# Down projection of 12 of 22 FFN pairs from seven block products instead of eight

## The chip, the cores and the metric

The kernel runs on one core of one Trainium2 chip. The metric is device time in microseconds (us) of one execution. The core has TensorE (PE in the profile; its weight loads are PEld), VectorE (DVE), ScalarE (ACT), GpSimd (POOL) and SyncE (SP). Each engine takes its own instructions in a fixed order and waits on semaphores for the others. DMAs are issued from SP's and from ACT's queue.

## The reference

One layer of an encoder block on 512 tokens of width 2048, all float32: an attention half (two branches, gates, output projection, LayerNorm) and a feed-forward half. The change is in the latter:

```python
h = modulate(layer_norm(x), shift2, scale2)
f = (jax.nn.silu(h @ w_ffn_gate[l]) * (h @ w_ffn_up[l])) @ w_ffn_down[l]
x = layer_norm_affine(DEEPNORM_ALPHA * x + gate2 * f, ln2_g[l], ln2_b[l])
```

Gate and up are 2048 x 5632, down is 5632 x 2048.

## The kernel before

**Split operands.** Each float32 operand is cut into a high part h (a cast to fp32r on ACT, line 95) and a low part l (the difference, on DVE, line 96). A product is three matmuls: h*h, h*l and l*h (`mm3`, lines 77 to 79). So every weight passes SP's DMA into a `raw` tile, a cast on ACT into a `wh` tile and a subtraction on DVE into a `wl` tile before TensorE can use it. `raw`, `wh` and `wl` have four buffers each, taken in turn.

**Gate and up.** The 5632 hidden columns are handled as 22 pairs of 128. For pairs 2 to 21 the products with gate and then with up are made by `strassen`, with seven block products in the place of eight (Winograd's form). A call has four steps (u = 0 to 3), each with 512 rows of weights, and a step has 42 matmuls of 128x256. The first 18 of them use raw blocks of the weights (tiles `hr`, `lr`, lines 1055 and 1056). The other 24 use sums of blocks, which POOL makes in a `tt` tile (lines 1058 to 1060) and which go through `wh` and `wl`. A pair has two calls, 336 matmuls. `combine` (lines 1088 to 1092) adds the products out of PSUM, on DVE but for one copy. After up, line 1138 multiplies silu(gate) by up into `eg` (128x1024: the pair's 256 hidden columns by 512 tokens), and `store_hid` writes that to DRAM from ACT's queue.

**Down.** Pairs 0 to 19 are taken in groups of four: `load_hid` loads a pair's hidden block again and splits it. For each of four column chunks of 512, four PSUM banks (one for each 128 tokens) collect the four pairs, 24 matmuls of 128x512 to a pair and chunk, so 96 to a pair. `drain` multiplies the bank by `gate2` and adds it to the residual `x2`. The last two pairs (N_LAST) have their weights multiplied by `gate2` beforehand, are kept split in SBUF, and run token block by token block, so that the final LayerNorm overlaps them.

**Order.** The program is written in sequence and a list scheduler, which runs a timeline of its own, then sets the order on each engine. That order is fixed when the kernel is built. An instruction behind another one on its engine waits for it.

## Time and profile before

| | |
|---|---|
| median of 3 runs | 2667.63 us (2666.36 to 2672.69) |
| the profiled execution | 2664.01 us, of which the profile's span is 2662.0 us |
| matmul instructions | 15563 |
| PE busy | 2592.6 us, 97% of the span |
| gate and up by seven products | from about 1360 to about 2165 us |
| down | from about 2165 us to the end |

Busy time of PE counts pipelined matmuls that overlap, so the share says where PE has no work, not how near it is to its peak. The rate of matmuls in a stretch says more: instructions of one shape at equal distances mean that nothing holds PE up. PE's clock as granted by the throttle is 1.00 (2.4 GHz) in nearly all slices.

### The profile page before, as it was taken

The page shows a single profiled execution, that of the slowest core. Times are in us where ns is not written, and L with a number is a line of the kernel's source. Part 1 is how long each engine was busy: PE and PEld are TensorE (multiplying, and loading weights), DVE is VectorE, ACT ScalarE, POOL GpSimd, SP SyncE. Part 2 cuts the span into 40 slices and gives each one's busy share as a digit, 9 for nine tenths or more (in the row PEclk, how much of TensorE's full clock was granted, in tenths as well). Part 3 has the DMA queues.
Part 4 walks back from the last instruction along what each step waited for, and adds up shares of the span by engine and source line. Part 5 has one row for each costly group of instructions (what it writes and reads, how often), then busy time and mean ns, then how long its engine had stood idle before and what let it go on. Part 6 is the DMA issues. An engine that isn't in the chain of part 4 may idle for free. (4 is left out here: it accounts for less than half of the span.)

```text
span 2662.0 us, 40015 instructions
## 1 busy us (share of the span) xinstructions
PE 2592.6 (97%) x15563; PEld 2314.5 (87%) x15563; DVE 1833.2 (69%) x2244; ACT 1012.9 (38%) x1456; POOL 1206.8 (45%) x1033
## 2 busy tenths in 40 slices
PE   5999999999989999999899999999999999999998
PEld 4888888789878888888899999999999998888886
DVE  8886787874678644577777677777777755445566
ACT  3332433333344533346644443444444432212321
POOL 0008778876745011020368777776677720000023
PEclk8999999999999999999999999999999999999999
DMA  9976578775734444768753333333333364334442
GB/s 350 320 256 211 156 228 254 244 246 173 237 101 151 129 144 142 240 217 260 238 166 120 118 120 119 115 120 124 111 120 123 116 214 150 119 110 128 151 127 87
DMA packets 330798, 456.11 MB, mean 171 GB/s; under 512 B 19656, under 2 KB 208480, under 8 KB 330096
## 3 DMA queue, kind: packets, MB, share of 16 engines
q1 hardware_dynamic: 307840, 414.77, 49.3%
q10 hardware_dynamic: 22768, 38.78, 4.1%
q8 instruction: 122, 2.00, 0.3%
q14 instruction: 68, 0.56, 0.1%
HBM read 418.87 MB, written 34.62 MB: 170 GB/s over the span
## 5 line engine op out<-in xcount | busy, mean ns | idle before, releaser
L96 DVE TENSOR_TENSOR wl<-raw,wh 128x1024 fp32r<-128x1024 f32 (+2 forms) x342 | 446.7, 1310 | 323.0 <-ACT wh L95 321.6
L95 ACT CAST wh<-raw 128x1024 fp32r<-128x1024 f32 (+2 forms) x342 | 346.3, 1015 | 706.9 <-PE ps_s L79 270.7
L96 DVE TENSOR_TENSOR wl<-tt,wh 128x1024 fp32r<-128x1024 f32 x160 | 235.7, 1474 | 168.3 <-ACT wh L95 168.1
L1058 POOL TENSOR_TENSOR tt<-raw 128x512 f32<-128x512 f32 x160 | 244.2, 1527 | 190.7 <-DMA raw<-in_w_ffn_up_dram 70.0
L95 ACT CAST wh<-tt 128x1024 fp32r<-128x1024 f32 x160 | 167.7, 1049 | 309.4 <-PE ps_s L78 134.5
L1056 DVE TENSOR_TENSOR lr<-raw,hr 128x768 fp32r<-128x768 f32 x160 | 215.4, 1346 | 44.7 <-ACT hr L1055 44.0
L230 POOL TENSOR_TENSOR acc<-acc,tmp 128x512 f32<-128x512 f32 (+1 forms) x154 | 207.3, 1346 | 9.8
L1208 POOL TENSOR_TENSOR raw<-raw,gate 128x512 f32<-128x512 f32 x16 | 25.3, 1609 | 400.9 <-DMA raw<-in_w_ffn_down_dram 400.9
L1055 ACT CAST hr<-raw 128x768 fp32r<-128x768 f32 x160 | 133.6, 835 | 151.0 <-PE ps_s L78 71.4
L226 POOL TENSOR_SCALAR tmp<-braw,csil 128x512 f32<-128x512 f32 x112 | 136.3, 1218 | 117.8 <-DMA braw<-in_w_ada_dram 114.4
L1060 POOL TENSOR_TENSOR tt<-raw,tt 128x256 f32<-128x256 f32 x160 | 174.5, 1092 | 11.7
L1059 POOL TENSOR_TENSOR tt<-raw,tt 128x256 f32<-128x256 f32 x160 | 170.6, 1067 | 11.7
L77 PE MATMUL ps_g<-hTh,wh 128*128 128x512 f32 x384 | 152.1, 397 | 1.7 <-ACT wh L95 1.7
L79 PE MATMUL ps_g<-hTh,wl 128*128 128x512 f32 x384 | 151.0, 394 | 0.0
L78 PE MATMUL ps_g<-hTl,wh 128*128 128x512 f32 x384 | 150.4, 392 | 0.0
L220 DVE SCALAR_TENSOR_TENSOR acc<-braw,csil,acc 128x512 f32<-128x512 f32 x112 | 112.6, 1006 | 43.4 <-DMA braw<-in_w_ada_dram 42.5
L77 PE MATMUL ps_s<-wh,hTh 128*128 128x512 f32 (+1 forms) x384 | 138.1, 361 | 0.0
L77 PE MATMUL ps_s<-sh,wh 128*128 128x256 f32 x480 | 135.2, 282 | 2.7 <-ACT wh L95 2.7
L79 PE MATMUL ps_s<-sh,wl 128*128 128x256 f32 x480 | 136.2, 284 | 1.4 <-DVE wl L96 1.4
L78 PE MATMUL ps_s<-wl,hTh 128*128 128x512 f32 (+1 forms) x384 | 137.5, 358 | 0.0
L79 PE MATMUL ps_s<-wh,hTl 128*128 128x512 f32 (+1 forms) x384 | 137.2, 358 | 0.0
L78 PE MATMUL ps_s<-sl,wh 128*128 128x256 f32 x480 | 136.3, 284 | 0.0
(432 smaller groups left out, 8251.5 us busy)
## 6 DMA issues: line engine op xcount, KB each, us to landing
braw<-in_w_ada_dram SPq DMA_DIRECT2D x128, 512.0 KB, 4.3
raw<-in_w_in_dram SPq DMA_DIRECT2D x96, 512.0 KB, 5.0
...
```

Source lines behind the costliest of these rows:

```text
L77: nc.tensor.matmul(ps, lhsT=ah, rhs=bh, start=start, stop=False)
L78: nc.tensor.matmul(ps, lhsT=ah, rhs=bl, start=False, stop=False)
L79: nc.tensor.matmul(ps, lhsT=al, rhs=bh, start=False, stop=stop)
L95: nc.scalar.copy(out=h[:, :n], in_=src)
L96: nc.vector.tensor_tensor(out=l[:, :n], in0=src, in1=h[:, :n], op=ALU.subtract)
L226: nc.gpsimd.tensor_scalar(out=dst[:, :n], in0=v[:, k, :], scalar1=col, scalar2=1.0, op0=ALU.mult, op1=ALU.mult)
L230: nc.gpsimd.tensor_tensor(out=acc2[:, :n], in0=acc2[:, :n], in1=dst[:, :n], op=ALU.add)
L1055: nc.scalar.copy(out=hr, in_=b[:, :, 1:4, :])
L1056: nc.vector.tensor_tensor(out=lr, in0=b[:, :, 1:4, :], in1=hr, op=ALU.subtract)
L1058: nc.gpsimd.tensor_tensor(out=t[:, :, 0:2, :], in0=b[:, :, 0:1, :].broadcast_to([P, 2, 2, P]), in1=b[:, :, 1:3, :], op=ALU.subtract)
L1059: nc.gpsimd.tensor_tensor(out=t[:, :, 2, :], in0=b[:, :, 2, :], in1=t[:, :, 0, :], op=ALU.subtract)
L1060: nc.gpsimd.tensor_tensor(out=t[:, :, 3, :], in0=b[:, :, 3, :], in1=t[:, :, 2, :], op=ALU.subtract)
```

## The change

**What it does.** Pairs 2 to 13 (`GROUPS`) leave the plain down projection. For them the down product too is made from seven block products: the pair's two blocks of 128 rows, two halves of the tokens and two halves of the output columns (each in two chunks c of 512) are the 2x2 blocks. That is 84 matmuls of 128x512 to a pair instead of 96. It runs over all 12 pairs in four passes: three of the seven products for c = 0, then for c = 1 (`weights1`, six PSUM banks, 18 matmuls to a pair), then the other four for c = 0 and c = 1 (`weights2`, eight banks, 24 matmuls to a pair). At the end of a pass the banks are added into the `x3` tiles without `gate2`; `convert` multiplies by `gate2` and adds the residual later. Pairs 0, 1 and 14 to 19 run as before in two groups (`PLAIN`), the last two as before.

**Weights.** Their block sums are made on DVE, in the loaded tiles: two additions of 128x512 for `weights1`, one of 128x1024 and one of 128x512 for `weights2`; then 1.5 or 2 splits of 128x1024 where a plain pair and chunk has one. Loads go alternately to `raw` tiles and to four new `tp` tiles.

**Activations.** After the multiplication (now line 1189) `hidden_sums` makes the four sums of hidden blocks on POOL (lines 1144 to 1147, into the `eu` tile), splits `eg` and the sums with the same `wh` and `wl` buffers as the weights, and stores the parts by eight DMAs from ACT's queue into `sets_d`. The down passes load them already split (`need1`, `need2`: 0.79 and 1.05 MB a pair) into a ring of 12 tiles.

```diff
+    GROUPS = [[2, 3, 4, 5, 6, 7, 8, 9, 10, 11, 12, 13]]
+    PLAIN = [[0, 1, 14, 15], [16, 17, 18, 19]]
...
+    def half_tile():
+        place[1] += 1
+        if extra_tiles and place[1] > RAW_ONLY and place[1] % 2:
+            return extra_tiles[0].tile([P, 1024], F32, tag="tp", name="tp", bufs=4)
+        return raw_tile()
...
+    def need1(g):
+        tl = set1[g] = ring_tile((3, g))
+        nc.sync.dma_start(out=parts(tl).bitcast(F32)[:, :, 0:768], in_=sets_d[g][:, :, 1024:1792])
...
+    def hidden_sums(g, eg, e):
+
+        nc.gpsimd.tensor_tensor(out=e[:, 0], in0=eg[:, 1], in1=eg[:, 2], op=ALU.subtract)
+        nc.gpsimd.tensor_tensor(out=e[:, 1], in0=e[:, 0], in1=eg[:, 3], op=ALU.subtract)
+        nc.gpsimd.tensor_tensor(out=e[:, 2], in0=eg[:, 3], in1=eg[:, 1], op=ALU.subtract)
+        nc.gpsimd.tensor_tensor(out=e[:, 3], in0=eg[:, 0], in1=e[:, 1], op=ALU.add)
+        for v, moves in ((eg, ((0, 0, 3, 2), (4, 3, 4, 1))), (e, ((2, 2, 4, 1), (5, 0, 2, 1)))):
+            for x, part in enumerate(split(v.rearrange("p b n -> p (b n)"), 1024)):
+                pb = part.bitcast(F32).rearrange("p (b n) -> p b n", b=4)
+                for to, b0, b1, st in moves:
+                    n = (b1 - b0 + st - 1) // st
+                    nc.scalar.dma_start(out=sets_d[g][:, x, to * 256:(to + n) * 256].rearrange("p (b n) -> p b n", b=n), in_=pb[:, b0:b1:st, :])
...
+    def weights1(g, c):
+        a, b = half_tile(), half_tile()
+        av, bv = a.rearrange("p (b n) -> p b n", b=2), b[:, :512]
+        nc.sync.dma_start(out=av, in_=w_rows(g, 0, c))
+        nc.sync.dma_start(out=bv, in_=w_rows(g, 1, c)[:, 1, :])
+        nc.vector.tensor_tensor(out=av[:, 1], in0=av[:, 1], in1=av[:, 0], op=ALU.add)
+        nc.vector.tensor_tensor(out=bv, in0=bv, in1=av[:, 1], op=ALU.add)
+        ah, al = split(a, 1024)
+        bh, bl = split(bv, 512)
...
         nc.vector.tensor_tensor(out=eg, in0=eg, in1=eu, op=ALU.mult)
-        store_hid(g, eg)
...
+        if g in by_sums:
+            hidden_sums(g, eg, eu)
+        else:
+            store_hid(g, eg)
...
-        return bank("ssssgtgt"[(turn8[0] - 1) % 8])
...
+        return bank("ssssggtt"[(turn8[0] - 1) % 8])
...
+    def weights2(g, c):
+        a, b = half_tile(), half_tile()
+        av, bv = a.rearrange("p (b n) -> p b n", b=2), b.rearrange("p (b n) -> p b n", b=2)
+        nc.sync.dma_start(out=bv, in_=w_rows(g, 0, c))
+        nc.sync.dma_start(out=av, in_=w_rows(g, 1, c))
+        nc.vector.tensor_tensor(out=bv, in0=bv, in1=av, op=ALU.add)
+        nc.vector.tensor_tensor(out=bv[:, 0], in0=bv[:, 0], in1=bv[:, 1], op=ALU.add)
+        ah, al = split(a, 1024)
+        bh, bl = split(b, 1024)
...
+    def products(pairs, sets, weights, c, step):
+        bk = None
+        for u, g in enumerate(pairs):
+            ws = ready.pop(0) if ready else weights(g, c)
+            if bk is None:
+                bk = [dbank() for _ in range(2 * len(ws))]
+            step(u, False)
+            for j, (b, w) in enumerate(ws):
+                for i in range(2):
+                    mm3(bk[2 * j + i], block(sets[g], b, i), w, u == 0, u == len(pairs) - 1)
+            step(u, True)
+        return bk
...
+            bk = products(pairs, set2, weights2, c, step)
+            for i in range(2):
+                add(nc.vector, z(0, 1, i, c), bk[i])
+            for i in range(2):
+                add(nc.vector, z(0, 0, i, c), bk[2 + i])
+            for i in range(2):
+                add(nc.vector, z(1, 0, i, c), bk[4 + i])
+                nc.vector.tensor_tensor(out=z(1, 1, i, c), in0=z(1, 1, i, c), in1=bk[4 + i], op=ALU.subtract)
+            for i in range(2):
+                add(nc.vector, z(1, 0, i, c), bk[6 + i])
```

**How it moves instructions.** The first place is ACT's queue where one pair's up call ends and the next pair's gate call begins (`eu` is the up result of the pair that ends; `hr` and `wh` from `tt` belong to the next pair's first steps). Before:

```order
L95 CAST wh_15146<-tt_15142 128x1024
L1055 CAST hr_15069<-raw_15067 128x768
L95 CAST wh_15202<-tt_15198 128x1024
L1055 CAST hr_15138<-raw_15136 128x768
L95 CAST wh_15258<-tt_15254 128x1024
L1088 COPY eu_15123<-ps_t_14898 128x256
L1055 CAST hr_15194<-raw_15192 128x768
L95 CAST wh_15314<-tt_15310 128x1024
L1055 CAST hr_15250<-raw_15248 128x768
L95 CAST wh_15380<-tt_15376 128x1024
L1016 DMA hid_d_88<-eg_14660 128x1024
```

The casts of the next pair's sums (`wh_15146`, `wh_15202`, `wh_15258`) stood ahead of the copy out of the pair's last PSUM banks. At the same boundary in the changed kernel:

```order
L1056 CAST hr_15234<-raw_15232 128x768
L1089 COPY eu_15200<-ps_t_14975 128x256
L1056 CAST hr_15290<-raw_15288 128x768
L1056 CAST hr_15346<-raw_15344 128x768
L95 CAST wh_15211<-eg_14737 128x1024
L1153 DMA sets_d_89<-wh_15211 128x2x256
L1153 DMA sets_d_89<-wh_15211 128x256
L1153 DMA sets_d_89<-wl_15212 128x2x256
L1153 DMA sets_d_89<-wl_15212 128x256
L95 CAST wh_15219<-eu_15200 128x1024
L95 CAST wh_15242<-tt_15238 128x1024
L95 CAST wh_15298<-tt_15294 128x1024
```

The next pair's first cast of sums (`wh_15242`) now stands behind the casts of `eg` and of the hidden sums (`wh_15211`, `wh_15219`), which read what line 1189 and POOL's four sums have written. DVE's order follows it: multiplication, `lr`, the two hidden subtractions, then the next pair's first `wl`. All 12 boundaries behind pairs 2 to 13 read alike; those behind pairs 14 to 20 keep the order of before.

The second place is PE at the same boundary. Before, from the last of the 18 matmuls on raw blocks:

```order
L77 MATMUL ps_s_15134<-sh_12208,hr_15138 128x256
L78 MATMUL ps_s_15134<-sl_12209,hr_15138 128x256
L79 MATMUL ps_s_15134<-sh_12208,lr_15139 128x256
L77 MATMUL ps_s_15133<-sh_12208,wh_15146 128x256
L78 MATMUL ps_s_15133<-sl_12209,wh_15146 128x256
L79 MATMUL ps_s_15133<-sh_12208,wl_15147 128x256
L77 MATMUL ps_s_15133<-sh_12208,wh_15146 128x256
L78 MATMUL ps_s_15133<-sl_12209,wh_15146 128x256
L79 MATMUL ps_s_15133<-sh_12208,wl_15147 128x256
```

The matmuls on sums follow in threes, each with its `wl`. In the changed kernel, from the same step on:

```order
L77 MATMUL ps_s_15231<-Mh0_10980,hr_15346 128x256
L78 MATMUL ps_s_15231<-Ml0_10981,hr_15346 128x256
L79 MATMUL ps_s_15231<-Mh0_10980,lr_15347 128x256
L77 MATMUL ps_s_15231<-Mh0_10980,hr_15346 128x256
L78 MATMUL ps_s_15231<-Ml0_10981,hr_15346 128x256
L79 MATMUL ps_s_15231<-Mh0_10980,lr_15347 128x256
L77 MATMUL ps_s_15229<-sh_12209,wh_15242 128x256
L78 MATMUL ps_s_15229<-sl_12210,wh_15242 128x256
L77 MATMUL ps_s_15228<-sh_12209,wh_15242 128x256
L78 MATMUL ps_s_15228<-sl_12210,wh_15242 128x256
L77 MATMUL ps_s_15230<-Ah0_10066,wh_15242 128x256
L78 MATMUL ps_s_15230<-Al0_10067,wh_15242 128x256
```

Here 12 matmuls on raw blocks of the next two steps (the six shown last, on `hr_15346`) are pulled ahead, so that 30 come before the first that needs a cast of sums, and then six that need only `wh_15242`, before the first that needs its `wl`. Again all 12 boundaries read so, and the other seven have 18 as before.

The third place is DVE at the end of the third down pass (c = 0 of `weights2`), where the next pass needs the same eight banks in the same order (`ps_g`, `ps_t`, `ps_s`). The banks' additions are lines 1252 and 1315; there is no such place before, where four banks were emptied while four others were filled:

```order
L1252 TENSOR_TENSOR x3_1_22468<-ps_t_23300,x3_1_22468 128x512
L1252 TENSOR_TENSOR x3_2_22469<-ps_s_23301,x3_2_22469 128x512
L1315 TENSOR_TENSOR x3_2_22469<-x3_2_22469,ps_s_23301 128x512
L1218 TENSOR_TENSOR raw_23886<-raw_23886 128x512
L96 TENSOR_TENSOR wl_23816<-tp_23809,wh_23815 128x1024
L1252 TENSOR_TENSOR x3_3_22470<-ps_s_23302,x3_3_22470 128x512
L1315 TENSOR_TENSOR x3_3_22470<-x3_3_22470,ps_s_23302 128x512
L1259 TENSOR_TENSOR x3_0_22467<-x3_0_22467,gate2_22474 128x2x512
L1259 TENSOR_TENSOR x3_1_22468<-x3_1_22468,gate2_22474 128x2x512
L1252 TENSOR_TENSOR x3_2_22469<-ps_s_23303,x3_2_22469 128x512
L96 TENSOR_TENSOR wl_23820<-raw_23810,wh_23819 128x1024
L1252 TENSOR_TENSOR x3_3_22470<-ps_s_23304,x3_3_22470 128x512
```

Between the additions stand splits and sums of the next pairs' weights (lines 96, 1217, 1218) and two multiplications by `gate2` (line 1259). Ahead of these rows, the first bank's addition is followed by a split and a sum (lines 96 and 1217) and then by those of the next two banks.

## Rows read from the trace of the kernel before

**Rows 1.** The page's busy line, then a line of its slices
```profile
PE 2592.6 (97%) x15563; PEld 2314.5 (87%) x15563; DVE 1833.2 (69%) x2244; ACT 1012.9 (38%) x1456; POOL 1206.8 (45%) x1033
...
PE   5999999999989999999899999999999999999998
```

**Rows 2.** Windows (us from the start); columns: length, busy (instructions) per engine, clock, DMA
```profile
1600.00:1800.00 200.00, 200.00 (x1671) 200.00 (x1671) 143.54 (x125) 82.63 (x95) 144.57 (x120) 1.00 0.37 117
2250.00:2350.00 100.00, 100.00 (x443) 82.81 (x442) 51.23 (x63) 22.88 (x22) 0.00 (x0) 1.00 0.37 116
```

**Rows 3.** Timeline of PE at the boundary of two pairs (start us, us)
```profile
1527.69 0.28 PE L79 MATMUL ps_t<-Mh,wl 128*128 128x256 f32 x1
1527.81 0.28 PE L77 MATMUL ps_s<-Ah,hr 128*128 128x256 f32 x1
...
1529.97 0.28 PE L77 MATMUL ps_s<-sh,wh 128*128 128x256 f32 x1
```

**Rows 4.** Timeline of DVE over the same boundary
```profile
1527.30 0.69 DVE L1089 TENSOR_TENSOR eu<-ps_g,eu 128x512 f32<-128x512 f32 x1 [0.46 <-PE ps_g L79]
...
1528.75 0.42 DVE L1091 TENSOR_TENSOR eu<-ps_g,eu 128x256 f32<-128x256 f32 x1
1529.09 1.62 DVE L96 TENSOR_TENSOR wl<-tt,wh 128x1024 fp32r<-128x1024 f32 x1
1530.64 0.68 DVE L1092 TENSOR_TENSOR eu<-ps_t,eu 128x512 f32<-128x512 f32 x1
1531.24 1.66 DVE L1056 TENSOR_TENSOR lr<-raw,hr 128x768 fp32r<-128x768 f32 x1
1532.82 1.76 DVE L1138 TENSOR_TENSOR eg<-eg,eu 128x1024 f32<-128x1024 f32 x1
...
1536.19 0.95 DVE L1056 TENSOR_TENSOR lr<-raw,hr 128x768 fp32r<-128x768 f32 x1
```

**Rows 5.** Timeline of POOL over the same boundary
```profile
1528.07 0.74 POOL L1059 TENSOR_TENSOR tt<-raw,tt 128x256 f32<-128x256 f32 x1
1528.89 0.74 POOL L1060 TENSOR_TENSOR tt<-raw,tt 128x256 f32<-128x256 f32 x1
1530.79 1.29 POOL L1058 TENSOR_TENSOR tt<-raw 128x512 f32<-128x512 f32 x1 [1.16 <-DVE wl L96]
1532.16 1.35 POOL L1059 TENSOR_TENSOR tt<-raw,tt 128x256 f32<-128x256 f32 x1
1533.58 1.60 POOL L1060 TENSOR_TENSOR tt<-raw,tt 128x256 f32<-128x256 f32 x1
```

**Rows 6.** Timeline of ACT over the same boundary
```profile
1532.98 1.05 ACT L95 CAST wh<-tt 128x1024 fp32r<-128x1024 f32 x1 [2.10 <-PE ps_s L78]
1534.62 0.33 ACTq L1016 DMA_DIRECT2D hid_d<-eg  x1
```

**Rows 7.** Groups by form, down stage (2180 to 2560 us)
```profile
L96 DVE TENSOR_TENSOR wl<-raw,wh 128x1024 fp32r<-128x1024 f32 x71 | 88.9, 1254 | 141.9 <-ACT wh L95 141.9
...
L1163 DVE TENSOR_TENSOR x<-x,dtmp 128x512 f32<-128x512 f32 x52 | 33.9, 682 | 0.0
...
L1158 DVE TENSOR_TENSOR dtmp<-ps_s,gate 128x512 f32<-128x512 f32 x36 | 23.5, 682 | 0.4
...
L1110 DVE TENSOR_TENSOR Ml<-raw,Mh 128x1024 fp32r<-128x1024 f32 x8 | 9.8, 1221 | 15.3 <-ACT Mh L1109 15.3
```

**Rows 8.** Windows of 5 us with two stops of PE, columns as in Rows 2
```profile
1300.00:1305.00 5.00, 2.44 (x20) 1.97 (x20) 3.44 (x5) 4.26 (x11) 0.00 (x0) 1.00 0.95 268
...
1310.00:1315.00 5.00, 2.42 (x18) 2.01 (x17) 0.00 (x0) 5.00 (x12) 0.66 (x1) 0.91 0.78 245
1315.00:1320.00 5.00, 3.32 (x15) 3.32 (x16) 4.87 (x7) 1.77 (x2) 0.75 (x2) 0.50 0.55 170
1320.00:1325.00 5.00, 5.00 (x40) 5.00 (x39) 3.09 (x4) 1.81 (x2) 1.44 (x2) 0.91 0.67 223
```

**Rows 9.** Window of the busiest transfers, columns as in Rows 2
```profile
60.00:80.00 20.00, 16.93 (x69) 13.76 (x70) 19.70 (x30) 7.55 (x12) 0.00 (x0) 0.91 1.06 377
```

More of the change, by code (lines that the diff above doesn't have):

```diff
@@ new lines, in block_kernel, with early @@
+    first = GROUPS[0]
+    ready = []
+    def early(u):
+        need1(first[u])
+        if u == 2:
+            ready.extend(weights1(first[v], 0) for v in range(2))
+    for g in range(N_SPLIT, N_PAIR):
+        eg = etile()
+        bk = strassen(w_ffn_gate, 2 * g, "ssss")
+        combine(eg, bk)
+        nc.scalar.activation(out=eg, in_=eg, func=AF.Silu)
+        bk = strassen(w_ffn_up, 2 * g, "ggtt", early if g == N_PAIR - 1 else None)
+        eu = sw.tile([P, 4, 256], F32, tag="eu", name="eu", bufs=1)
+        combine(eu, bk)
+        nc.vector.tensor_tensor(out=eg, in0=eg, in1=eu, op=ALU.mult)
+        if g in by_sums:
+            hidden_sums(g, eg, eu)
+        else:
+            store_hid(g, eg)
@@ new lines, in block_kernel, with tick @@
+    later = []
+    LAG = 3
+    def tick(fn):
+        later.append(fn)
+        if len(later) > LAG:
+            f = later.pop(0)
+            if f is not None:
+                f()
+    def products(pairs, sets, weights, c, step):
[10 more added lines that the diff above has]
+        return bk
@@ L1179, in down @@
                 for t in range(NT):
                     for k in range(2):
-                        mm3(bb[t], hid[u].at(k, t), pair(hl, slice(None), k), u == 0 and k == 0, u == n - 1 and k == 1)
-            if extra is not None:
-                extra(cc)
-            for t in range(NT):
-                drain(bb[t], t, cc, first_)
-    g0 = 0
-    for gi in range(4):
-        hid = first_hid if gi == 0 else [load_hid(g0 + i, *hid_slot(4 * (gi % 2) + i)) for i in range(GROUP)]
-        down(g0, hid, gi == 0)
-        g0 += GROUP
@@ L1192, in block_kernel @@
-    pop("sw", "left")
-    hp = push("hp", "left")
-    def hp_hid(g):
-        return load_hid(g, hp.tile([P, 4, 256], F32R, tag="hh", name="hh", bufs=6), hp.tile([P, 4, 256], F32R, tag="hl", name="hl", bufs=6))
+                        mm3(bb[t], plain_hid[g].at(k, t), pair(hl, slice(None), k), u == 0 and k == 0, u == len(pairs) - 1 and k == 1)
+                if todo:
+                    todo.pop(0)()
+                if n == 3:
+                    vacate((0, g))
+                tick(following.pop(0) if following and n == 3 else None)
@@ new lines, in block_kernel, with load_affine, fn @@
+    g2, b2 = [], []
+    def load_affine(dst, src):
+        def fn():
+            tl = ring_tile(("affine", id(dst)), F32)
+            for j in range(4):
+                dst.append(tl[:, j, :])
+                nc.sync.dma_start(out=tl[:, j, :], in_=src[0, j * 512:(j + 1) * 512].partition_broadcast(P))
+        return fn
+    queue = [lambda g=g: load_hid(g) for grp in PLAIN + [[gl, gl + 1]] for g in grp]
+    queue += [load_last(cc, u) for cc in range(4) for u in range(N_LAST)]
+    queue += [load_affine(g2, ln2_g), load_affine(b2, ln2_b)]
@@ new lines, in block_kernel @@
+    for gi in range(len(GROUPS)):
+        if gi + 1 < len(GROUPS):
+            left = strassen_down(gi, [lambda g=g: need1(g) for g in GROUPS[gi + 1]])
+            assert not left
+        else:
+            spare = len(RING) - len(GROUPS[gi])
+            for f in queue[:spare]:
+                tick(f)
+            queue = strassen_down(gi, queue[spare:])
+    if PLAIN:
+        todo = [lambda c=c, t=t: convert(c, [t]) for c in range(2) for t in range(NT)]
+        for grp in PLAIN:
+            queue = down(grp, (0, 2, 1, 3), queue, todo)
@@ L1221, in block_kernel @@
+    while later:
+        f = later.pop(0)
+        if f is not None:
+            f()
+    for f in queue:
+        f()
+    if not PLAIN:
+        convert(1)
     for t in range(NT):
```

203 lines of the change are left out of this document (129 added, 74 removed).

## Prediction

> **What bounds the kernel now.** I read the page's busy line and slices first: PE is busy for 97% of the span, and its slices stand at 9 from the second on [rows 1]. That can hide waits, so I read the rate of matmuls next. In the gate and up stage 1671 matmuls of 128x256 start in 200 us, 0.1197 us each. In the down stage 443 of 128x512 start in 100 us, 0.2257 us each. Both stretches have the full clock and PE busy throughout [rows 2]. VectorE has 72% of the first and 51% of the second, and the transfers a third. So in both stages the number of matmuls sets the time, and everything else is free as long as its result is there in time. Whether it is there is read at the boundary of two pairs, in the timelines of four engines. There PE passes from the last matmul of a pair's up call (1527.69) to the next pair's first (1527.81, called E below) without a gap, and comes to the first matmul that needs a cast of sums (`wh`) at 1529.97, 2.16 us behind E [rows 3].
>
> **What goes.** Twelve pairs have 84 matmuls in down instead of 96: 144 x 0.2257 = 32.5 us less of PE. The twelve loads and splits of `load_hid` for these pairs lay beside PE and give nothing back.
>
> **What comes at the pairs' boundaries.** This is the largest term. Before, three casts of the next pair's sums stood ahead of the boundary. Now the first of them stands on ACT behind the cast of the hidden sums, and that is the end of a chain that starts only when PE has finished the pair:
> - VectorE's additions out of PSUM run at 1527.30, 1528.03 and 1528.75 and leave it free at 1529.09 [rows 4]. The fourth now follows at once (before, a split stood between): 0.68, to 1529.8. The multiplication took 1.76 with POOL at work beside it [rows 4]. POOL's sums for the next two steps are done by then and its queue waits for this very result, so I take 1.22, what DVE's 128x1024 takes with POOL idle [rows 7]: 1531.05.
> - POOL's four sums of 128x256: 0.74 each alone, 0.08 from one to the next [rows 5], 3.2 in all. But DVE's `lr` and `wl` of `eg`, with two inputs from SBUF, run beside them. In such company the same POOL operation took 1.35 and 1.60 [rows 5], and `lr` 1.66 instead of 0.95 [rows 4]. With two of four so slowed, 4.7 us: 1535.8. ACT's cast of `eg` and its first four DMAs (0.33 each) are over by then.
> - ACT: the cast of the sums, 1.05 [rows 6], to 1536.95, then that of the next pair's first step, to 1538.0.
> - DVE: the subtraction for the hidden sums and then the first `wl`, 1.22 each [rows 7]: 1538.2 and 1539.45, which is E + 11.65.
>
> By then PE has had work for 30 matmuls on raw blocks and six that need only the cast, 36 x 0.1197 = 4.3 us. So it loses 7.3 us to each boundary. With nothing contending the sums end at 1534.1, the second `wl` at 1538.0 after the DMA issues, and the loss is 5.9; with three of four sums slowed and the DVE work beside them slowed too it is 8.2. It does not come back: PE is the bound of the stage before and after, and the buffers are full again two steps on (POOL's next sums start when `wl` frees their tile, and are split some 8 us later, about when PE needs them).
>
> The Trainium skill (SBUF — State Buffer, Who interferes with whom) says that VectorE with two inputs from SBUF contends with GpSimd's reads, and that whoever issues first holds the shared port for the whole instruction while the other is blocked. The rows of POOL and DVE above agree in kind; by the rule at full strength the upper figure would hold, without it the lower.
>
> PE stands still for some 5 us at a time. What that does to its clock: a stop of 2.56 us in 1300 to 1305 left it at 1.00, one of 2.58 us in 1310 to 1315 was followed by 0.50 (1.2 GHz) in the next 5 us, and 0.91 in those behind [rows 8]. With 3.32 us busy in the first of these and 0.91 worth 0.9 us at half in the second, PE worked some 4.2 us at half and lost 2.1. Here the six matmuls at the start run while `wl` is awaited anyway, which hides 0.7 of it. Between 0 and 2.1 I take 1.2 for each boundary, nearer the row with the drop since the stop is twice as long.
>
> The Trainium skill (TensorE: Matmul & The Clock Gate, HAM oscillation — how this bites in real kernels) says that a loop which leaves TensorE waiting in each turn pays the cold clock in each turn. One of the two stops above agrees and one does not; by the rule all twelve boundaries would pay.
>
> Sum: 12 x (7.3 + 1.2) = 102 us. Bounds 12 x 5.9 = 71 and 12 x (8.2 + 2.1) = 124.
>
> **What comes in the down passes.** VectorE first. For `weights1` a pair has two additions of 128x512 (0.68), a split of 1.22 and one of 0.68: 3.3 us beside 18 x 0.2257 = 4.1 us of PE. For `weights2` 1.22 + 0.68 + 2 x 1.22 = 4.3 beside 5.4 [rows 7]. That is 80%, with POOL idle, so hidden between the ends of passes. At the end of the third pass the next needs each bank 0.68 us after the one before, and emptying one costs DVE 0.68 [rows 7], twice that for two banks, with the splits and multiplications between. Following the order from the first bank (done 4.75 us ahead of the pass's end): the first `s` bank is free 1.1 us behind the end and needed at 2.7, but the second at 5.0 (needed 3.4), the third at 8.2 and the fourth at 10.1, each setting the next back. PE loses 5.3 us. Bounds: 0, if splits come late and additions go first, and 12, if none of DVE's work is done ahead and the clock falls. The other passes rotate to free banks, and I cost them at nothing; the cover is two pairs of finished weights.
>
> Transfers: while the second pass loads both weights (0.79 MB) and the next set (1.05 MB) for each 4.1 us, 450 GB/s are asked for. The most in rows is 377 [rows 9]. So loads fall behind by 0.8 us a pair for seven pairs, but each is issued five or six pairs ahead. Nothing.
>
> In the gate and up stage each of the 12 pairs gets two more casts and eight DMA issues on ACT (4.7 us of 40), two subtractions on DVE and four sums on POOL, all idle for over a fifth of the time [rows 2]. These cost nothing but for their place.
>
> **Sum.** Profiled execution 2664.0 (span 2662.0 and 2.0 around it) - 32.5 + 102 + 5.3 = 2738.8 us. That execution lies 3.6 below the median of the runs shown, 2667.6, so for a median I say 2742 us.
>
> **Rivals.**
> 1. *The stall is as short as it can be, and the clock holds.* 12 x 5.9: 2667.6 - 32.5 + 71 + 5.3 = 2711. For it: POOL has nothing else queued; one stop in the trace did not cost the clock. Against: `lr` is released just as POOL starts. 17%.
> 2. *The stall is long, and the clock falls fully at each.* 12 x 10.3 = 124, with a third step that is late by up to 1 us: 2667.6 - 32.5 + 124 + 12 + 7 = 2778 at most. 13%.
> 3. *The down passes are bound by loads or by DVE too.* If the lead of five pairs does not cover it, loads cost 0.8 x 7 = 6 us, at the share now seen (116 GB/s at 0.37, so 313 when full) 1.8 x 9 = 16: 2748 to 2758. For it: 450 GB/s asked. Against: the lead of 20 us. 8%.
> 4. *The other side: the boundary is covered.* The gain of 32.5 less 5.3 is eaten by a loss of 2.3 us at each of 12 boundaries, so by a first `wl` at E + 6.6; earlier than that the kernel is faster, at best 2667.6 - 32.5 + 5.3 = 2640. For it: the scheduler has pulled work ahead there. Against: what it pulled ahead is 4.3 us, and the chain's operations alone, each at its least, add up to over 10. 7%.
>
> The forecast has the other 55%.
>
> **How the numbers follow.** 2742 is the likeliest. The range goes from rival 1 with nothing lost in the passes, 2667.6 - 32.5 + 71 = 2706, widened to 2700, to the upper bounds 2667.6 - 32.5 + 124 + 12 = 2771, widened to 2776. It leaves out rival 4 and the end of rival 2. About 0.3% (8 us) is what a measurement here can tell from no change. Only rival 4 gives anything but slower: faster 0.05, within 0.3% 0.02, slower 0.93.
>
> **What would show it.** In the changed profile, from pair 2's end: pairs 48 to 49 us apart for twelve boundaries (now 40.2) and 40.2 for the last seven; PE waiting there for ACT's cast and DVE's `wl`, 60 to 80 us in sum; the granted clock under 1.00 in windows behind the stops; the multiplication at 1.22; the hidden sums at 0.7 to 1.6. In the down passes one wait of some 5 us, on DVE's addition at line 1252 or 1315, and matmuls otherwise 0.2257 apart. I am wrong if pairs 2 to 13 are 40 to 42 us apart, or if PE waits in the down passes for transfers or weights by more than 15 us.

## The result and the profile after

The changed kernel takes 2744.1 us (median of 4 runs, 2740.1 to 2745.4); beside it the kernel before took 2669.6 (4 runs). The ratio is 1.0284, 95% interval 1.0271 to 1.0296: 2.8% slower. The profiled execution took 2740.12 us with a span of 2738.3. The page's busy line and the slices that answer to [rows 1]:

```profile
PE 2594.2 (95%) x15419; PEld 2308.9 (84%) x15419; DVE 1915.0 (70%) x2340; ACT 1057.4 (39%) x1516; POOL 1264.8 (46%) x1073
...
PE   5999999999899999999889898998999999999998
```

144 matmuls are gone, yet four of PE's digits between 1370 and 1920 us are 8, none before. The windows that answer to [rows 2] (us, then busy time and instructions of PE, PEld, DVE, ACT, POOL, then clock, DMA share, GB/s):

```profile
1600.00:1800.00 200.00, 176.54 (x1382) 173.31 (x1380) 116.42 (x115) 73.74 (x86) 133.93 (x113) 0.92 0.39 124
2300.00:2340.00 40.00, 40.00 (x178) 33.14 (x177) 35.34 (x49) 19.95 (x26) 0.00 (x0) 1.00 0.81 279
```

In the gate and up stage 1382 matmuls start in 200 us, where 1671 did, at a clock of 0.92. In the down stage 178 start in 40 us, 0.2247 us each, as before. So the loss lies in the first stage. One boundary of two pairs there, in PE's timeline, which answers to [rows 3] (E = 1601.19):

```profile
1601.08 0.28 PE L79 MATMUL ps_t<-Mh,wl 128*128 128x256 f32 x1
1601.19 0.28 PE L77 MATMUL ps_s<-Ah,hr 128*128 128x256 f32 x1
...
1605.99 0.28 PE L79 MATMUL ps_s<-Mh,lr 128*128 128x256 f32 x1
1611.29 0.58 PE L77 MATMUL ps_s<-sh,wh 128*128 128x256 f32 x1 [5.02 <-ACT wh L95]
```

PE goes through its 30 matmuls on raw blocks and then waits 5.02 us for ACT's cast of the next pair's first sums. What ACT waits for is read back through DVE, POOL and ACT, the rows that answer to [rows 4 to 6]:

```profile
1603.39 1.23 DVE L1189 TENSOR_TENSOR eg<-eg,eu 128x1024 f32<-128x1024 f32 x1
1604.53 0.95 DVE L1057 TENSOR_TENSOR lr<-raw,hr 128x768 fp32r<-128x768 f32 x1
1605.72 1.43 DVE L96 TENSOR_TENSOR wl<-eg,wh 128x1024 fp32r<-128x1024 f32 x1 [0.24 <-ACT wh L95]
1610.33 1.23 DVE L96 TENSOR_TENSOR wl<-eu,wh 128x1024 fp32r<-128x1024 f32 x1 [3.17 <-ACT wh L95]
1611.47 2.35 DVE L96 TENSOR_TENSOR wl<-tt,wh 128x1024 fp32r<-128x1024 f32 x2
```

```profile
1604.69 1.38 POOL L1144 TENSOR_TENSOR eu<-eg 128x256 f32<-128x256 f32 x1 [6.99 <-DVE eg L1189]
1606.03 1.70 POOL L1146 TENSOR_TENSOR eu<-eg 128x256 f32<-128x256 f32 x1
1607.70 0.72 POOL L1145 TENSOR_TENSOR eu<-eu,eg 128x256 f32<-128x256 f32 x1
1608.49 0.72 POOL L1147 TENSOR_TENSOR eu<-eg,eu 128x256 f32<-128x256 f32 x1
```

```profile
1609.25 1.04 ACT L95 CAST wh<-eu 128x1024 fp32r<-128x1024 f32 x1 [3.56 <-POOL eu L1147]
1610.20 1.04 ACT L95 CAST wh<-tt 128x1024 fp32r<-128x1024 f32 x1
```

Multiplication, four hidden sums (two of them about twice as long as the others), the cast of the sums, and only then `wh<-tt`, done at E + 10.05. The first `wl` is done near E + 11.5. The clock behind the stop, in windows of 5 us that answer to [rows 8]:

```profile
1600.00:1605.00 5.00, 4.73 (x38) 4.32 (x36) 4.33 (x7) 1.19 (x2) 0.31 (x1) 1.00 0.35 105
1605.00:1610.00 5.00, 0.74 (x4) 0.54 (x4) 1.91 (x2) 1.44 (x2) 4.14 (x4) 0.77 0.47 157
1610.00:1615.00 5.00, 3.71 (x18) 3.62 (x19) 3.50 (x3) 2.19 (x3) 2.23 (x2) 0.55 0.56 210
1615.00:1620.00 5.00, 5.00 (x44) 5.00 (x44) 1.54 (x2) 2.15 (x3) 4.71 (x5) 1.00 0.09 18
```

It is near half speed (1.2 GHz) when PE works again, and full in the next window. From 10 to 15 us behind E it is 0.50 to 0.67 at each of the twelve boundaries and 1.00 at the other seven.

For the sums that follow I take the start of each pair (its first gate matmul) from PE's timeline. Before, pairs start 40.27 us apart. After, the twelve behind pairs 2 to 13 start 48.4 to 49.6 apart, one more 41.8, the last six 40.27. Twelve pairs take 104.1 us more than 12 x 40.27, 1.5 of which the kernel before loses too in its first. The down stage (first to last 128x512 matmul) goes from 478.5 to 450.8 us. 102.6 + 1.5 (the thirteenth) - 27.7 = 76.4 is the difference of the two spans, 76.3.

### The profile page after: what moved, and what is told of

Same layout as the page of the kernel before. It is cut to its first block, busy times and chain, and to the rows that moved or that the text cites. A ratio compares the mean times of both kernels' runs of the same rounds, so it can differ in the third digit from the quotient of the medians.

```text
span 2738.3 us, 40126 instructions
## 1 busy us (share of the span) xinstructions
PE 2594.2 (95%) x15419; PEld 2308.9 (84%) x15419; DVE 1915.0 (70%) x2340; ACT 1057.4 (39%) x1516; POOL 1264.8 (46%) x1073
## 4 chain that ended last, share of the span: by engine, by line
PE 41%; POOL 4%; DVE 3%; ACT 1%; issue 1%; DMA 1%; POOLq 0%; SPq 0%; ACTq 0%; DVEq 0%
PE ps_s L77 7%; PE ps_s L79 7%; PE ps_s L78 7%; PE ps_g L78 4%; PE ps_g L79 4%; PE ps_g L77 4%; PE ps_t L78 3%; PE ps_t L79 3%; PE ps_t L77 3%; ACT wh L95 1%; POOL tt L1059 1%; POOL eu L1146 1%; POOL eu L1144 1%; DVE eg L1189 1%; POOL tt L1060 1%
## 5 line engine op out<-in xcount | busy, mean ns | idle before, releaser
L95 ACT CAST wh<-raw 128x1024 fp32r<-128x1024 f32 (+2 forms) x345 | 338.8, 985 | 630.1 <-PE ps_s L79 218.3
L1059 POOL TENSOR_TENSOR tt<-raw 128x512 f32<-128x512 f32 x160 | 290.4, 1825 | 156.6 <-DVE wl L96 125.5
L96 DVE TENSOR_TENSOR wl<-tt,wh 128x1024 fp32r<-128x1024 f32 x160 | 217.1, 1376 | 158.2 <-ACT wh L95 157.9
L1057 DVE TENSOR_TENSOR lr<-raw,hr 128x768 fp32r<-128x768 f32 x160 | 207.4, 1297 | 117.6 <-ACT hr L1056 117.1
L77 PE MATMUL ps_s<-sh,wh 128*128 128x256 f32 x480 | 145.9, 305 | 62.3 <-ACT wh L95 62.3
L1060 POOL TENSOR_TENSOR tt<-raw,tt 128x256 f32<-128x256 f32 x160 | 162.4, 1025 | 5.3
L77 PEld LDWEIGHTS ps_s<-sh,wh 128*128 128x128 f32 x480 | 100.8, 210 | 65.2 <-ACT wh L95 65.2
L1061 POOL TENSOR_TENSOR tt<-raw,tt 128x256 f32<-128x256 f32 x160 | 146.3, 925 | 5.3
L78 PE MATMUL ps_s<-sl,wh 128*128 128x256 f32 x480 | 143.9, 301 | 0.0
L79 PE MATMUL ps_s<-sh,wl 128*128 128x256 f32 x480 | 141.9, 304 | 1.4 <-DVE wl L96 1.4
L1367 POOL TENSOR_TENSOR tp<-tp,gate 128x1024 f32<-128x1024 f32 x5 | 17.0, 3402 | 271.1 <-DMA tp<-in_w_ffn_down_dram 265.8
```

Of the source, the lines that this page charges most:

```text
L77: nc.tensor.matmul(ps, lhsT=ah, rhs=bh, start=start, stop=False)
L78: nc.tensor.matmul(ps, lhsT=ah, rhs=bl, start=False, stop=False)
L79: nc.tensor.matmul(ps, lhsT=al, rhs=bh, start=False, stop=stop)
L95: nc.scalar.copy(out=h[:, :n], in_=src)
L96: nc.vector.tensor_tensor(out=l[:, :n], in0=src, in1=h[:, :n], op=ALU.subtract)
L1057: nc.vector.tensor_tensor(out=lr, in0=b[:, :, 1:4, :], in1=hr, op=ALU.subtract)
```

## Experiments

Theory: the loss at the boundaries is the place of the hidden work in the queues of ACT and VectorE, ahead of what PE needs next, and the clock. Rivals: the added work as such (load, above all GpSimd's), the wait for buffers, and GpSimd working against VectorE. The measure is the excess: the time of the 12 pairs over 12 x 40.27, read as above in the one profiled execution of each kernel. The times are medians, with the number of executions; a single one has no interval.

| kernel | us | excess of 12 pairs, us |
|---|---|---|
| before | 2669.6 (4) | 1.5 |
| changed | 2744.1 (4) | 104.1 |
| e1_later | 2675.6 (6 runs) | 34.5 |
| e2_dve | 2732.7 (1) | 91.2 |
| e3_nosums | 2678.6 (1) | 38.0 |
| e4_spread | 2671.8 (10) | 34.2 |
| e5_no_sums_spread | 2648.0 (1) | 7.2 |
| e6_vector_spread | 2662.7 (1) | 21.7 |
| e7_in_order | 2679.6 (6) | 38.8 |
| e8_up_call | 2675.5 (6) | 32.8 |
| e9_up_call_vector | 2656.1 (4) | 14.5 |
| e10_sums_twice | 2711.9 (1) | 74.2 |
| e11_vector_late | 2669.5 (11) | 30.7 |
| e12_first_free | 2654.1 (5) | 16.1 |

### The same work, one step later: e1_later

```diff
+    def run_waiting(u):
+        if u == 0 and waiting:
+            waiting.pop()()
-        bk = strassen(w_ffn_gate, 2 * g, "ssss")
+        bk = strassen(w_ffn_gate, 2 * g, "ssss", run_waiting)
-            hidden_sums(g, eg, eu)
+            waiting.append(lambda g=g, eg=eg, eu=eu: hidden_sums(g, eg, eu))
```

> The same work as the changed kernel, but the hidden sums, their splits and stores of a pair are written one step later in the program: behind the second step's weight sums of the next pair's gate call. In the built order ACT then has the next pair's first two casts of sums ahead of the boundary and only the third behind the two hidden casts; PE has 18 matmuls on raw blocks at each boundary as before, none pulled ahead. Theory (place in the queues): the hidden chain is the same, cast of the sums done at about E + 10.1 (as measured in the changed kernel), then the third step's cast at E + 11.2 and its wl at E + 12.6; PE reaches it after 84 + 18 matmuls, 12.2 us, so it loses 0 to 1 us to each of 12 boundaries in the place of 8.55: 2744 - 12 x 8 = about 2648 us, range 2637 to 2656, pairs 40.3 to 41.3 apart. Rival (load): if the added work of POOL, DVE, ACT or the DMAs itself held PE up, it would stay at 2735 to 2745, pairs 48 to 49 apart, since none of it is taken away. A rival that allows half, the buffers wh and wl being held by the eight stores: about 2700.

Measured: 2675.6, ratio to before 1.0036 (1.0021 to 1.0051), pairs 43.1 apart. Two thirds of the loss go with the place alone. But 34.5 us stay, against the 0 to 12 that I expected. The wait for `wh` at the boundary is down to 0.23; PE now waits elsewhere, in its first step, for `lr`:

```profile
1624.15 0.38 PE L79 MATMUL ps_s<-Ah,lr 128*128 128x256 f32 x1 [1.61 <-DVE lr L1057]
...
1636.62 0.39 PE L77 MATMUL ps_s<-sh,wh 128*128 128x256 f32 x1 [0.23 <-ACT wh L95]
```

The chain of work that ended last, from 1450 to 1850 us of e1, says who holds it up. Before, PE makes up all of it; here GpSimd (POOL) makes up 79% and PE nothing:

```profile
by line: POOL tt L1059 33.9%; POOL tt L1060 19.3%; POOL tt L1061 14.6%; DVE wl L96 9.6%; ACT wh L95 7.2%; POOL eu L1146 4.2%; issue 4.2%; POOL eu L1144 3.5%; POOL eu L1147 1.9%; POOL eu L1145 1.7%; POOLq L1059 0.2%; DVEq L1057 0.1%
```

### The chain, link by link: e2_dve and e3_nosums

e2: `nc.gpsimd` becomes `nc.vector` in the four sums of `hidden_sums`. e3:

```diff
-        nc.gpsimd.tensor_tensor(out=e[:, 0], in0=eg[:, 1], in1=eg[:, 2], op=ALU.subtract)
...
-        for v, moves in ((eg, ((0, 0, 3, 2), (4, 3, 4, 1))), (e, ((2, 2, 4, 1), (5, 0, 2, 1)))):
+        for v, moves in ((eg, ((0, 0, 3, 2), (4, 3, 4, 1), (2, 2, 4, 1), (5, 0, 2, 1))),):
```

> The four hidden sums are made on VectorE in the place of GpSimd, everything else stays. Theory (the chain's length, by the built order of DVE: multiplication, lr, two sums, wl of eg, two sums, wl of the sums, wl of the next pair's first step): multiplication done at E + 3.4, lr 0.95, two sums of 0.42, wl 1.22, two sums of 0.42 (durations of the forms in the trace without contention), so sums done at E + 7.3 in the place of E + 8.0; cast of the sums and of the first step 2.1: first wh at E + 9.4 (E + 10.05 in the changed kernel), first wl at E + 10.7. The loss goes down by 0.7 us to each boundary only: about 2744 - 8 = 2736 us, range 2727 to 2741. Rival (GpSimd's added work and its contention with VectorE is the cause): the sums no longer load GpSimd nor run against it, so most of the 102 us goes: 2640 to 2680.

> The four hidden sums and the split of their tile are left out; all seven stored blocks of a pair are taken from the split of eg, so the output is not the layer's. The place of the one split left stays as it is, with the stores behind the next casts. Theory: the chain is multiplication (done E + 3.4), cast of eg (E + 4.55), first wh of the next pair (E + 5.6), and on DVE lr, wl of eg, wl of the first step (E + 7.1). PE has 3.6 us on raw blocks, waits 2.0 for the cast, works 0.7 and waits another 0.7: 2.8 us to each boundary, 34 us in the place of 102.6, and with stops of at most 2 us little or no drop of the clock: 2744 - 69 = 2675 us, range 2664 to 2690, pairs about 43.1 apart. If the clock falls at each boundary all the same, 1 us more for each: 2687. Rival (the place in the queues does not matter, the stores or the splits' load do): eg's split and all eight stores' bytes remain, so half or more of the 102 us stays: 2695 or more.

Measured: 2732.7 and 2678.6. Both fall within what the chain gives. In e2 the first `wh` of the next pair was done at E + 9.05 (E + 9.4 expected), in e3 at E + 5.45 (5.6), and PE then lost 3.2 us a pair in place of 2.8. GpSimd freed of the sums did not help in e2: at this place it is the length of the chain that counts, not whose work it is. The stores of a pair's seven blocks remain in e3, so the buffers that they hold are not the cause of the 66 us that went.

### The same work in three parts: e4_spread, e5_no_sums_spread, e6_vector_spread

```diff
+        def one():
+            ab()
+            out((eg, ((0, 0, 3, 2), (4, 3, 4, 1))))
+        return [one, cd, lambda: out((e, ((2, 2, 4, 1), (5, 0, 2, 1))))]
...
-            hidden_sums(g, eg, eu)
+            waiting.extend(hidden_sums(g, eg, eu))
...
-                            nc.scalar.dma_start(out=gate2[:, cs], ...
+                            nc.sync.dma_start(out=gate2[:, cs], ...
```

`ab` and `cd` are two sums each, `out` splits and stores; one part runs behind each step of the next pair's gate call. In e5 `ab` and `cd` are empty, in e6 they are on `nc.vector`.

> The same work as the changed kernel, with the hidden work in three parts in the next pair's gate call: two sums and the split of eg behind the second step's weight sums, two sums behind the third's, the split of the sums behind the fourth's. In the built order the third step's cast now stands ahead of the cast of the hidden sums. The four gate2 loads in the first down pass go from ACT's queue to SP's. Theory: nothing that PE needs waits for the hidden sums, so pairs come 40.3 apart and the 102.6 us go; the gate2 move gives back the 2.4 us at the start of the first down pass: 2744 - 105 = 2639 us, range 2633 to 2648, which is faster than the kernel before by some 28 us (1%). Rival (load): 2735 to 2745. If the third step's cast is late by up to 1 us at each boundary: 2651.

> As e4_spread, but GpSimd's four hidden sums are left out (the tile that they fill is split and stored as it stands, so the output is not the layer's); both casts, both subtractions and all eight stores of a pair remain. In e4_spread pairs 2 to 13 still come 41.3 to 44.3 apart, 42.7 on the mean, 29 us more than 12 times 40.27. Theory (the loop): GpSimd's weight sums stand two steps together in its queue and wait for the wl that frees their tile; from one such pair of steps to the next 8.8 to 9.4 us pass, where PE takes 10.07. The four hidden sums put 5.2 to 6.4 us into that loop once for each pair, and the slack of four turns gives back only some 2.7 to 5 of it. Without the sums pairs come 40.3 to 40.6 apart: 2672 - 29 = 2643 us, range 2637 to 2650. Rival (the two added casts and subtractions in the order of ACT and VectorE, or the stores, hold PE up): at least half of the 29 us stays, 2657 or more.

> As e4_spread, with the four hidden sums made on VectorE. Theory (the loop): GpSimd's loop is as if there were no sums, VectorE gets four instructions of 0.4 us for each pair, 1.7 us of 40, which is also in that loop but is less than its slack of 0.7 to 1.2 us in each of four turns: pairs 40.3 to 41.3 apart, 2643 to 2655 us, I say 2647. Rival (the added work of VectorE is what holds PE up, since it is busy for over 75% there): slower than e4_spread, 2675 to 2690.

Measured: 2671.8 (ratio 1.0017, 1.0007 to 1.0026), 2648.0 and 2662.7. e4 missed: the excess is 34, as in e1, at another wait (`lr` in the up call, 19 us in all). e5 says of what: without GpSimd's four sums, with both splits and all stores left, 27 of the 34 go. With the sums on VectorE (e6) 12.5 go; its time lies between what I expected and the rival. The gate2 move is not shown to be worth anything: PE's lag behind an even pace at the start of the first pass is 1.5 us in e4, 2.4 in the changed kernel, but 1.5 in e1 too, where the loads were not moved.

### GpSimd's order or its load: e7_in_order, e8_up_call, e10_sums_twice

```diff
-        nc.gpsimd.tensor_tensor(out=t[:, :, 0:2, :], ...)
+        tc.keep_in_program_order(nc.gpsimd.tensor_tensor(out=t[:, :, 0:2, :], ...))
...
+    def run_gate(u):
+        if u >= 2 and waiting:
+            waiting.pop(0)()
+    def run_up(u):
+        if waiting:
+            waiting.pop(0)()
```

All GpSimd sums, of weights and hidden, are so held. In e8 `run_gate` does nothing (`u >= 9`). e10 is e8 with the four lines of hidden sums doubled.

> All the work of the changed kernel, with the hidden sums on GpSimd. GpSimd's weight sums keep the order of the program, step by step (each behind the one before), so that one tile's sums are made while the other's cast and subtraction run. The first two hidden sums and the split of eg stand behind the fourth step's weight sums of the next pair's gate call, the other two sums behind the second step's of its up call, the split of the sums behind the third's. ACT then has the next pair's first three casts of sums ahead of the boundary, as in the kernel before. gate2's loads are on SP's queue as in e4_spread. Theory (the loop, and the place): a step takes GpSimd 3.2 to 3.8 us, eight steps and the hidden sums 32 to 37 of 40.27, with no wait for wl between two steps of one tile's turn: pairs 40.3 apart from the first boundary on, and 2744 - 102.6 - 2.4 = 2639 us, range 2634 to 2648. This is faster than the kernel before by 1.1%. Rival (GpSimd's load as such): with the hidden sums still there, pairs stay 42 to 43 apart: 2660 to 2673.

> As e7_in_order, with every part of the hidden work one call later in GpSimd's order: the first two sums and the split of eg behind the second step's weight sums of the next pair's up call, the other two sums behind the third's, the split of the sums behind the fourth's. In e7_in_order GpSimd stood 55.3 us of a stretch of 400 us waiting for the multiplication (5 us of each pair, its weight sums queued behind the waiting hidden sum), and was busy for 341.3 of the 400. Theory (the wait in GpSimd's queue): its work is 341.3 / 9.2 pairs = 37.1 us a pair, under the 40.27 that PE needs; e7 was slow because 37.1 and 5 are more than 40.27. Without the wait pairs come 40.3 to 41 apart: 2639 us, range 2634 to 2652, faster than the kernel before by about 1%. Rival (GpSimd is too slow in itself, its instructions stretched by VectorE's work beside them): 42 to 44 us for a pair as before, 2660 to 2680.

> As e8_up_call, but each of GpSimd's four hidden sums is made twice (the same result). In e8_up_call pairs come 43.0 apart, with nothing waiting for the hidden sums, GpSimd busy for 358.5 of 400 us, and PE waiting for lr on VectorE, 0.5 to 2.1 us at a time. Theory (GpSimd's throughput is the second limit, once the place is right): four more sums of 0.74 to 1.46 us, as they took in e8, lengthen each of 12 pairs by 3.0 to 4.7 us: 2675 + 36 to 56 = 2711 to 2731, pairs 46 to 47.7 apart. Rival (VectorE's order alone makes lr late, GpSimd has 10% to spare): pairs 43.0 to 43.6, 2675 to 2682.

Measured: 2679.6 (1.0043, 1.0027 to 1.0060), 2675.5 (1.0027, 1.0016 to 1.0039), 2711.9. e7 missed by 40 us: the loop of two steps that I had blamed was taken apart, and nothing was gained. In its timeline GpSimd stood 5 us in each pair, its queue held by the first hidden sum:

```profile
1632.64 1.33 POOL L1061 TENSOR_TENSOR tt<-raw,tt 128x256 f32<-128x256 f32 x1
1638.99 0.74 POOL L1145 TENSOR_TENSOR eu<-eg 128x256 f32<-128x256 f32 x1 [5.02 <-DVE eg L1210]
```

So I formed the theory that this wait was the loss. e8 took it away, and missed as well: 6 us gained, 33 left, as its rival said. e10 then showed that GpSimd's time itself counts: four more sums cost 3.45 us a pair ((74.2 - 32.8) / 12), about what they take. The same window of before, of e8 and of e10:

```profile
1450.00:1850.00 400.00, 400.00 (x3340) 400.00 (x3339) 284.65 (x249) 165.67 (x190) 294.00 (x241) 1.00 0.38 119
```

```profile
1450.00:1850.00 400.00, 378.41 (x3105) 373.71 (x3104) 291.63 (x250) 163.89 (x195) 358.51 (x259) 1.00 0.43 138
```

```profile
1450.00:1850.00 400.00, 368.60 (x2913) 364.39 (x2912) 273.41 (x234) 154.33 (x183) 357.61 (x274) 0.95 0.41 130
```

POOL (the last busy figure) is at 90% and 89%: times the mean pair (43.0 and 46.45) that is 38.5 and 41.5 us a pair, where it was 29.6 before. The remaining tenth it waits for the `wl` that frees a `tt` tile:

```profile
L1059 POOL TENSOR_TENSOR tt<-raw 128x512 f32<-128x512 f32 x75 | 140.9, 1879 | 32.0 <-DVE wl L96 31.8 <-DMA raw<-in_w_ffn_up_dram 0.2
L1060 POOL TENSOR_TENSOR tt<-raw,tt 128x256 f32<-128x256 f32 x74 | 102.9, 1391 | 5.8
...
L1149 POOL TENSOR_TENSOR eu<-eg 128x256 f32<-128x256 f32 x9 | 13.1, 1454 | 0.0
L1145 POOL TENSOR_TENSOR eu<-eg 128x256 f32<-128x256 f32 x9 | 6.7, 747 | 0.0
```

Behind that wait stand, in part, the hidden stores. Once a pair ACT's cast waits some 3 us for a store that holds its `wh` buffer:

```profile
ACT wh L95 <- DMA sets_d<-wh: 30.4, 10, 4.7
```

e1 has no such wait at an excess of 34.5, so it isn't needed for the loss; what it adds in e8 to e12 is untested, since no run gives the casts more buffers.

So GpSimd's `tt` loop is part of the second limit. The sums themselves are under 4 us (0.75 + 0.75 + 1.45 + 0.73); the rest of the added 8.9 is that the weight sums became longer, 1.39 us in place of 1.05 for the second of a step, beside more work on VectorE (why is said further down).

### The four sums on VectorE: e9_up_call_vector, e11_vector_late, e12_first_free

e9 is e8 with the four hidden sums on `nc.vector`, not held to an order. e11 also holds them, and holds GpSimd's weight sums only from pair 3 on; e12 has only the latter:

```diff
+        keep = tc.keep_in_program_order if f0 > 2 * N_SPLIT else (lambda ins: ins)
-        tc.keep_in_program_order(nc.gpsimd.tensor_tensor(...))
+        keep(nc.gpsimd.tensor_tensor(...))
...
-            nc.vector.tensor_tensor(out=e[:, 0], ...)
+            tc.keep_in_program_order(nc.vector.tensor_tensor(out=e[:, 0], ...))
```

> As e8_up_call, with the four hidden sums on VectorE, which the built order puts right behind the multiplication, between the weights' subtractions, none of which is pulled into groups of two. GpSimd then has only the weight sums in the program's order, as in the kernel before (294 of 400 us busy there). Theory (a wait or a loop on GpSimd is what is left, VectorE has room): VectorE gets 2 x 1.22 + 4 x 0.42 = 4.1 us a pair, 285 + 41 = 326 of 400 us; pairs 40.3 apart, 2637 us, range 2632 to 2645. Rival (VectorE's added work delays lr and wl as in e6_vector_spread, where PE waited 1.7 us a pair for lr): pairs 41 to 42, 2648 to 2662.

> As e9_up_call_vector, with VectorE's four hidden sums held to their place in the program as well (two behind the second step's subtraction of the next pair's up call, two behind the third's, not right behind the multiplication), and GpSimd's weight sums held to the program's order only from pair 3 on. In e9_up_call_vector pairs came 41.5 apart on the mean, PE waiting 0.8 us a pair for lr in the gate call, and 4.7 us were lost in the first pair, where the weight sums stood behind the tokens' sums. Theory (what is left is work on VectorE ahead of lr at the boundary): pairs 40.3 to 41.0, so 6 to 14 us less, and the first pair's 4.7 us back: 2656 - 16 = 2640 us, range 2634 to 2648. Rival (VectorE's instructions are stretched by GpSimd's beside them, wherever they stand): pairs stay 41.3 to 41.6, 2649 to 2654. The 5.3 us that e9 lost at the end of its fourth down pass, where a load of weights came late, may stay or go in either: another 5 us.

> As e9_up_call_vector in all but one thing: GpSimd's weight sums are held to the program's order from pair 3 on, not from pair 2 on. e11_vector_late had this and VectorE's sums held to a later place, and was slower than e9 by 13 us; this run tells the two apart. Theory A (the later place of VectorE's sums cost it: the subtractions of eg and of the sums took 1.7 to 1.8 us there and 1.21 in e9, and the sums and weight sums beside them were slow as well): this one keeps e9's pace, pairs 41.2 to 41.7, and gains 1 to 5 us in the first pair: 2651 to 2656, I say 2653. Theory B (the order in the first pair decides how GpSimd and VectorE fall together in all that follow): pairs 42.5 or more, 2664 to 2672.

Measured: e9 2656.1, ratio to before 0.9954 (0.9937 to 0.9970); e11 2669.5, 1.0003 (0.9994 to 1.0012); e12 2654.1, 0.9954 (0.9941 to 0.9968). e9 and e12 beat both kernels, the one before by 0.5% (small, but both intervals lie below 1) and, by the ratios, the changed one by 3.2%. For e9 that is 19 us short of what I expected, inside its rival's range. e12 came out in sum as expected, but not in its parts: its first pair lost 5.5 us where I had expected a gain on e9, and a loss of e9's in the down stage did not recur. e11 was a miss: the later place made the sums' neighbours longer and the pairs 42.8. e12 puts that down to VectorE's order (theory A), not to the first pair. In e12 the subtractions of `eg` and `eu` take 1.21 us, in e11 1.81 and 1.72. In the rows of e12 three of the four sums pay for their place, right behind the multiplication, while GpSimd is at work:

```profile
L1211 DVE TENSOR_TENSOR eg<-eg,eu 128x1024 f32<-128x1024 f32 x10 | 17.6, 1757 | 0.0
L1146 DVE TENSOR_TENSOR eu<-eg 128x256 f32<-128x256 f32 x10 | 14.0, 1402 | 0.3
...
L1150 DVE TENSOR_TENSOR eu<-eg 128x256 f32<-128x256 f32 x10 | 9.6, 955 | 0.0
L1151 DVE TENSOR_TENSOR eu<-eg,eu 128x256 f32<-128x256 f32 x10 | 9.5, 954 | 0.0
L1147 DVE TENSOR_TENSOR eu<-eu,eg 128x256 f32<-128x256 f32 x10 | 4.1, 412 | 0.0
```

What makes up e12's last 16 us of excess was not taken apart. Two of the twelve pairs hold 10 of it (45.7 and 45.1 us apart), and PE waits 9.8 us in all for `lr`.

## Why the prediction was right, and where it was not

**What goes.** 144 x 0.2267, the distance of the matmuls in this trace, is 32.6 us: right.

**The boundaries.** Forecast 102 (7.3 for the chain and 1.2 for the clock at each of twelve), measured 102.6. The order read in ACT's queue gave the chain, and the durations of [rows 4 to 7] its length: the multiplication 1.23 (1.22 said), the four sums with their gaps 4.5 (4.7), the first `wh` done at E + 10.05 (E + 10.2). At each of the twelve PE is 7.2 us late when its first `wl` comes (7.3 said). The clock then costs 0.8 to 2.1 us more, 1.4 on the mean, so its term of 1.2 was a little small; it is 0.8 at the boundary shown. Twelve times 7.2 and 1.4 make the 104 of the table, 1.5 of which the kernel before loses too. The clock's term was read from two stops of [rows 8] that were two waits each: the one that left the clock at 1.00 is 1.82 and 0.74 us, and the one followed by 0.50 is 1.44 us and one of 2.83 that runs on into the next window:

```profile
1303.52 0.66 PE L929 MATMUL ps_t<-ident,xn 128*128 128x128 f32 x4 [1.82 <-ACT mt L933]
...
1316.68 0.58 PE L78 MATMUL ps_s<-Ml,wh 128*128 128x256 f32 x1 [2.83 <-DVE Ml L942]
```

That 1.2 came near was in part luck. That the loss is the chain of the hidden sums is shown by e2 and e3: shortened by about 1 and about 4.6 us, it gave back 1.1 and 5.5 us a pair, the latter with a smaller loss by the clock. PE's waits from pair 2 to the down stage are the forecast's 60 to 80 us:

```profile
PE ps_s L77 <- ACT wh L95: 62.3, 14, 5.0
PE ps_s L79 <- DVE lr L1057: 9.5, 13, 1.0
```

The Trainium skill (TensorE: Matmul & The Clock Gate, HAM oscillation — how this bites in real kernels) says that a loop which leaves TensorE waiting in each turn pays the cold clock in each turn. The trace agrees: 0.50 to 0.67 behind all twelve stops of some 5 us.

**The step that failed: "These cost nothing but for their place."** I had costed the hidden sums on POOL, the casts, subtractions and DMA issues at nothing, since all these engines were idle for over a fifth of the time [rows 2]. In the changed kernel that was true only because PE's stop gave them room: GpSimd was busy for 269.1 of 400 us, less than before. Once the place is mended (e1, e4, e7, e8), 33 to 39 of the 104 us remain. e5 shows that 27 of e4's 34 go with GpSimd's sums, e10 that more sums cost more. So none of these versions comes to the 2640 us of rival 4; the best with all the work is 2654, with the sums on VectorE. The forecast's time was right without this, because the longer stall covers the shorter one.

GpSimd alone is not the bound either: in e9 it has no hidden sums and is busy for 320.5 of 400 us, VectorE for 326.9, and pairs are still 41.5 us apart. The rows show what I had overlooked: of these two engines, the one that starts second takes longer by what the other's instruction still has to run, less some 0.13 us, while the one that started first keeps its time. At the boundary shown, `wl<-eg` starts with 0.35 us of L1144 to run and takes 1.43 in place of 1.22; L1146 starts with 1.12 us of that `wl` to run and takes 1.70 in place of 0.72. VectorE's additions out of PSUM are spared (0.68 us beside GpSimd too). So the two engines' times add up, and idle shares of over a fifth were no measure of room.

An estimate of the sum for a pair uses the durations without company (GpSimd 1.29 for 128x512 and 0.74 for 128x256; VectorE 1.22 for 128x1024, 0.95 for 128x768, 0.41 for 128x256). Before, a pair has 8 x (1.29 + 2 x 0.74) on GpSimd and 8 x (1.22 + 0.95) + 1.22 on VectorE; the change adds two subtractions of 1.22 and the four sums:

| | sum, us | pairs apart, us |
|---|---|---|
| before | 40.7 | 40.3 (PE's own pace) |
| no sums (e5) | 43.2 | 40.9 |
| sums on VectorE (e6, e9, e11, e12) | 44.8 | 42.1, 41.5, 42.8, 41.6 |
| sums on GpSimd (e1, e4, e7, e8) | 46.1 | 43.1, 43.1, 43.5, 43.0 |
| sums twice (e10) | 49.1 | 46.5 |

Every version but the first lies 2.0 to 3.3 us below its sum, so the kernel before had next to no room left. This fits all ten, with the sums' place and engine changed, but no run was made to test it.

The Trainium skill (SBUF — State Buffer, Who interferes with whom) has VectorE and GpSimd exclude each other on a shared port. The rows agree: what the second engine loses is nearly all that is left of the other's instruction.

**The down passes.** Forecast a loss of 5.3 us, all at the end of the third pass; measured about 4.9 (32.6 - 27.7), most of it elsewhere. There VectorE does empty the banks as late as I said, the last 10.06 us behind the pass's end (2442.20):

```profile
2449.85 0.68 DVE L1252 TENSOR_TENSOR x<-ps_s,x 128x512 f32<-128x512 f32 x1
...
2451.58 0.68 DVE L1252 TENSOR_TENSOR x<-ps_s,x 128x512 f32<-128x512 f32 x1
```

But PE lost only 0.5 there. I had followed VectorE's order and not PE's, which has later pairs' products on free banks pulled ahead. Half of the loss, 2.4 us, came at the start of the first pass, where I had costed nothing. There ACT's queue was held by three of the four gate2 loads, and the cast behind them was late:

```profile
2276.21 6.68 ACTq L1278 DMA_DIRECT2D gate<-rows_d  x3
2283.06 1.05 ACT L95 CAST wh<-raw 128x1024 fp32r<-128x1024 f32 x1 [6.26 <-DMA gate<-rows_d]
```

But only 0.4 us of PE's loss follows right on that cast, and e1, which leaves these loads where they are, loses 1.5 there, as much as e4, which moved them. So the cause of the 2.4 us stays open. That the sum came out near was chance.

**Transfers.** Nothing, as forecast, behind the start of the first pass: from there to the end of the second PE kept its pace, though the transfers moved more than in the window of [rows 9]:

```profile
2340.00:2400.00 60.00, 60.00 (x264) 48.96 (x263) 44.44 (x52) 23.14 (x29) 0.00 (x0) 1.00 1.04 397
```

In e9 a late load of weights, with ACT's queue behind it, did cost about 5 us at the end of the fourth pass; it did not recur in e12.
